# A mixture-of-experts stage on one Trainium2 core: narrow slots' tokens in one shared tile, a tenth ring buffer for weights, and block transposes placed behind the splits

## The chip, the cores and the metric

One core of one Trainium2 chip runs the whole program. The metric is device time in microseconds (us) of that core, from one launch; lower is better. PE is TensorE's matmuls, DVE is VectorE, ACT is ScalarE, SP issues nearly all transfers, POOL is idle in what follows.

## The reference, cut to what matters

Two layers of a trunk, 256 tokens of width 1024. The second layer ends in a mixture of eight experts, of which each token uses two:

```python
logits = (t @ w_router) + b_router
top_val, top_idx = lax.top_k(logits, 2)
top_w = jax.nn.softmax(top_val, axis=-1)
for e in range(8):
    out += combine[:, e:e+1] * ((silu(t @ w_gate[e]) * (t @ w_up[e])) @ w_down[e])
```

Each expert has a gate and an up matrix of 1024 x 3584 and a down matrix of 3584 x 1024, all f32. They are 352 MB together, of 470 MB that the kernel reads, and each weight is read once.

## The kernel before, in words

Everything up to the router runs first (some 520 us). Then comes the expert stage, written in one fixed order by hand, which each engine follows in program order.

**Slots and units.** Experts are ranked by how many tokens chose them. Eight slots hold them; `CAPS = (3, 4, 3, 3, 3, 2, 2, 2)` is the room of each slot in groups of 32 tokens. A slot's expert is cut into seven chunks of 512 hidden columns; one slot with one chunk is a *unit*. Slots run in two lanes, (0, 1, 2, 3) and (5, 6, 4, 7), whose units alternate. So slot 1 alternates with the last units of slot 5 and the first of slot 6.

**Pieces.** A unit needs four *pieces* of gate and up weights and two of down weights. A piece is 128 x 2048 f32, 1 MB, loaded by one DMA issue on SP (L137). The down matmuls of a unit (`ps_d`) stand on PE behind the gate and up matmuls (`ps_gu`) of the next unit.

**Narrow and wide.** Seven slots are *narrow* (2 or 3 groups). They stream the raw f32 pieces through PE in 32-column tiles (L1090). Slot 1, with 4 groups, is *wide*: each piece is first split into two fp32r parts, `hi` by a copy on ACT (L146) and `lo = raw - hi` by a subtraction on DVE (L154). Three matmuls then take each step: `hi` with both halves of the tokens (L260, L261), `lo` with one (L262). There are three `hi` and three `lo` buffers. A call `ahead(2)` behind the unit in front splits the first two pieces; the third and the fourth are split as the unit's own matmuls reach them.

**Between `ps_gu` and `ps_d`** a unit computes `sg = silu(gate)` on ACT (L1121) and `mh = up * sg` on DVE (L1124), and turns `mh` round: `h_T`. A narrow unit does that with 16 block transposes of 32 x 32 blocks on DVE (L1135), a wide one with four matmuls on PE (L1139). When a slot is done, `gated` scales its sums (`yg` on DVE L1173, `yhi` on ACT L1175, `ylo` on DVE L1176), and `combine` scatters them back (`ps_sc`, L1200).

**Where pieces land.** `need` loads pieces in the order of a plan. `mk` chooses the buffer of each. Nine `raw` buffers form a ring. Where no wide piece is within some items of the plan, the `hi` and `lo` buffers hold raw pieces too, 15 in all. Near the wide slot only the nine remain, and SP's next issue waits for the piece nine places before it to be used up (a narrow piece by its matmuls, a wide one by its `lo`).

**The 8 KB tiles.** Four buffers `a8` (8 KB on each partition) hold the gathered tokens of the slots at work (`xn` narrow, `xg` wide) and the running sum `macc`.

Of the kernel before, what the change touches and what calls it, by code (L numbers as in the profile page):

```python
# [17 lines left out]
P = 128  # L18
# [3 lines left out]
KT = 8  # L22
# [14 lines left out]
CAPS = (3, 4, 3, 3, 3, 2, 2, 2)  # L37
LANES = (0, 1, 2, 3), (5, 6, 4, 7)
STAGGER = 3
NR = NE - 1  # L40
EPS = 1e-6
NORM = D ** 0.5 / -8192.0
NEG = -1e30
G = 2048
# [9 lines left out]
def kernel(ctx, tc, x, cvec, wada, bada, wga, wqkv, wout, wfgu, wfd, wfd2,  # L54
# [5 lines left out]
    rawp = ctx.enter_context(tc.tile_pool(name="raw", bufs=RAW))  # L60
# [96 lines left out]
    plan = []  # L157
# [27 lines left out]
    def wide(e):  # L185
        return CAPS[e] == 4
# [9 lines left out]
    plan.append(down_chunk(*units[-1]))  # L196
    halves = [(k, s) for k, (_, n) in enumerate(plan) for s in range(0, n, G)]
    limit = [sum(k < first_gu for k, _ in halves)]
    raws, his, los, used = [], [], [], [0]

    def need(k):
        while len(raws) <= min(k, len(plan) - 1):
            i = len(raws)
            ap, n = plan[i]

            def mk(h):
                m = 2 * (i - first_gu) + h
                if m in SPARE8:
                    return pools["wk"], "a8", G
                if m in SPARE4:  # L210
                    return pools["wk"], "a4", G // 2
                if i >= first_gu and not any(n_ for _, n_ in plan[i - 6:i + 3]):
                    at = m % 15
                    return ((rawp, "raw", G), (hip, "hi", G), (lop, "lo", G))[(at >= 9) + (at >= 12)]
                return rawp, "raw", G

            raws.append(load(ap() if callable(ap) else ap, n or 4096, mk))

    def ahead(nhi, nlo=None, pre=True):

        for _ in range(nhi):
            if len(his) < limit[0]:
                k, s = halves[len(his)]
                need(k + pre)
                his.append(half_hi(raws[k], s))
            else:
                need(len(raws) + pre)
        for _ in range(nhi if nlo is None else nlo):
            if len(los) < limit[0]:
                k, s = halves[len(los)]  # L230
                los.append(half_lo(raws[k], s, his[len(los)]))
# [681 lines left out]
    def moe(acc, g_bc, mm, A, B, AW, bw):  # L913
# [45 lines left out]
        def shares():  # L959

            w0 = const.tile([P, NT], F32, name="w0")
            w1 = const.tile([P, NT], F32, name="w1")
            nc.vector.tensor_tensor(w1, m8[:, :, 1], m8[:, :, 0], op=ALU.subtract)
            nc.scalar.activation(w1, w1, AF.Exp)
            nc.vector.tensor_scalar(w0, w1, 1.0, None, op0=ALU.add)
            nc.vector.reciprocal(w0, w0)
            nc.vector.tensor_tensor(w1, w1, w0, op=ALU.mult)
            for t in range(NT):
                nc.vector.tensor_scalar(comb[:, t, :], oh[:, 1, t, :], w1[:, t:t + 1], None, op0=ALU.mult)
                nc.vector.scalar_tensor_tensor(comb[:, t, :], oh[:, 0, t, :], w0[:, t:t + 1], comb[:, t, :],  # L970
                                               op0=ALU.mult, op1=ALU.add)
# [67 lines left out]
        def dispatch(e, pm):  # L1039


            g, n = CAPS[e], 32 * CAPS[e]
            src, at = (gates, places) if e else (comb, posm)
            if wide(e):
                xg = a8("xg", [P, 2, KT, P], F32R)

                def put(js, f):
                    nc.scalar.activation(xg[:, 0, js, :], f, AF.Copy)
                    nc.vector.tensor_tensor(xg[:, 1, js, :], f, xg[:, 0, js, :].bitcast(F32), op=ALU.subtract)
            else:  # L1050
                xg = a8("xn", [P, KT, n])

                def put(js, f):
                    nc.vector.tensor_copy(xg[:, js, :], f)

            gather(pm, n, put)
            ps = bank("ps_ws")
            ws = sm.tile([P, 4], F32, tag="ws", name="ws")

            for tt in range(NT):  # L1060
                nc.tensor.matmul(ps[:, tt * P:(tt + 1) * P], at[:, tt, e:e + 1].to_broadcast([P, P]), ident,
                                 start=True, stop=True)
            if wide(e):
                for tt in range(NT):
                    nc.tensor.matmul(ps[:, S:S + 1], pm[:, 0, tt, :], src[:, tt, e:e + 1], start=tt == 0,
                                     stop=tt == NT - 1)
                pT = a4("pmT", [P, S], F32R)
                nc.vector.tensor_scalar(pT, ps[:, 0:S], spot[:, 0:1], None, op0=ALU.is_equal)
                nc.vector.tensor_copy(ws[:, 0:1], ps[:, S:S + 1])
                return xg, pT, ws  # L1070
            for t in range(g):
                for tt in range(NT):
                    for j in range(4):
                        nc.tensor.matmul(ps[32 * j:32 * j + 32, S + t:S + t + 1], pm[:, 0, tt, 32 * t:32 * t + 32],
                                         src[:, tt, e:e + 1], start=tt == 0, stop=tt == NT - 1)
            pT = a4("pmT", [P, g, S], F32R)
            for t in range(g):
                nc.vector.tensor_scalar(pT[:, t, :], ps[:, 0:S], spot[:, 4 + t:5 + t], None, op0=ALU.is_equal)
            nc.vector.tensor_copy(ws[:, 0:g], ps[:, S:S + g])
            return xg, pT, ws  # L1080
# [212 lines left out]
            nc.gpsimd.memset(room[:, at[0]:at[-1] + 1], 32.0 * v)  # L1293
        pm = slot_pick(0)
        shares()
        disp, accs = {0: dispatch(0, pm)}, {}
        idx_i, over_i = rank()
        ada_through(len(ada_order))
# [3 lines left out]
        with tc.manual_schedule():  # L1302
            limit[0] = len(halves)
            for r in range(NR):
                order[r + 1] = nc.values_load(idx_i[0:1, r:r + 1], engines=[mybir.EngineType.SP], min_val=1, max_val=NR,
                                              skip_runtime_bounds_check_because="a rank's expert")
            g2r = const.tile([P, 256], F32, tag="crep", name="g2r")
            pend, done = None, []
            for n, (e, c) in enumerate(units):
                early = [(pe, gated(pe)) for pe in done]  # L1310
                done = []
                if c == N_DN - 2 and e in after:
                    nxt = after[e]
                elif n == STAGGER - 1:
                    nxt = LANES[1][0]
                else:
                    nxt = None
                if nxt is not None:
                    pm = slot_pick(nxt)

                def between():
                    if pend and wide(pend[0]):
                        ahead(2)

                hm = gu_mm(e, between)
                if n == 1:
                    g2_bc = bcast(vec(1, 5), "g2bc")
                    dgs = [a2("dg", [P, 4, P]) for i in range(2)]
                    for i, dg in enumerate(dgs):
                        nc.vector.tensor_tensor(dg, ident[:, None, :].to_broadcast([P, 4, P]),  # L1330
                                                vec(1, 5)[:, 4 * i:4 * i + 4, None].to_broadcast([P, 4, P]), op=ALU.mult)
                    ps = bank("ps_g2")
                    for j in range(4):
                        nc.tensor.matmul(ps[32 * j:32 * j + 32, 0:256], ones_1[:, 0:32],
                                         dgs[j // 2][:, 2 * (j % 2):2 * (j % 2) + 2, :].rearrange("p a s -> p (a s)"),
                                         start=True, stop=True)
                    nc.scalar.activation(g2r, ps[:, 0:256], AF.Copy)
                for pe, ys in early:
                    if pe == 0:
                        macc = a8("macc", [P, NT, D])  # L1340
                    combine(pe, ys)
                if pend is not None:
                    if pend[1] == 0:
                        accs[pend[0]] = [accbank(f"ps_d{b}") for b in range((CAPS[pend[0]] + 1) // 2)]
                    dn_mm(*pend)
                    if pend[1] == N_DN - 1:
                        done.append(pend[0])
                if n + 1 < len(units) and wide(units[n + 1][0]):
                    ahead(2)
                pend = e, c, h_T(hm, CAPS[e], wide(e))  # L1350
                if nxt is not None:
                    disp[nxt] = dispatch(nxt, pm)
            for pe in done:
                combine(pe, gated(pe))
            dn_mm(*pend)
            combine(pend[0], gated(pend[0]), store)
# [164 lines left out]
```

## Time and profile before

| | before |
|---|---|
| median of 3 runs | 1393.73 us (1391.57 to 1395.06) |
| the profiled execution | 1396.89 us, of which the span of its instructions is 1395.2 us |
| PE busy, of the span | 1322.7 us (95%) |
| DVE / ACT busy | 772.2 us (55%) / 371.5 us (27%) |
| transfers | 473.64 MB, mean 339 GB/s |
| chain that ended last | PE 81%, DVE 8%, DMA 6%, ACT 4% |
| mean granted clock of PE | 0.983 |

Times in rows are us from the start of the span. The outside of the span is 1.7 us. Busy shares are means over stages with different limits, so the rows further down are taken stage by stage.

### The profile page before, as it was taken

How to read it: one execution, taken by the hardware profiler on the slowest of the kernel's cores; microseconds unless marked ns; L12 is line 12 of the kernel's file. 1: busy time of each engine (PE TensorE's matmuls, PEld its weight loads, DVE VectorE, ACT ScalarE, POOL GpSimd, SP SyncE). 2: the span in 40 equal slices, each digit the busy share in tenths (PEclk: the TensorE clock that was granted, in tenths of full speed). 3: DMA queues.
4: the chain of work that ended last, by engine and by line, in shares of the span. 5: the costliest groups of instructions: out<-in, count | busy, mean ns of one | idle time of the engine just before them, and what ended most of it. 6: DMA issues, size and time to landing. Idle time of an engine off the chain costs nothing.

```text
span 1395.2 us, 38875 instructions
## 1 busy us (share of the span) xinstructions
PE 1322.7 (95%) x17220; PEld 974.2 (70%) x17220; DVE 772.2 (55%) x1832; ACT 371.5 (27%) x574; POOL 3.1 (0%) x18
## 2 busy tenths in 40 slices
PE   4998999999899999999899999999999999999996
PEld 4877689999788676666567666766765776666663
DVE  3498677777689855343566565653344343334253
ACT  3336443443455430101234333410000100100000
POOL 0000000000000000000000000000000000000000
PEclk9999999999999999999999999999999999999999
DMA  9962787888461469899879999999999999999995
GB/s 387 399 276 91 262 305 275 307 300 300 161 237 59 151 218 401 353 424 424 344 309 423 387 373 371 367 413 424 424 425 424 424 424 424 396 418 418 423 424 215
DMA packets 66383, 473.64 MB, mean 339 GB/s; under 512 B 7840, under 2 KB 7968, under 8 KB 9248
## 3 DMA queue, kind: packets, MB, share of 16 engines
q1 hardware_dynamic: 66208, 471.09, 83.9%
q8 instruction: 137, 2.24, 0.6%
q14 instruction: 38, 0.31, 0.1%
HBM read 470.01 MB, written 1.05 MB: 338 GB/s over the span
## 4 chain that ended last, share of the span: by engine, by line
PE 81%; DVE 8%; DMA 6%; ACT 4%; issue 1%; SPq 0%; ACTq 0%; DVEq 0%
PE ps_gu L1090 28%; PE ps_d L1090 14%; PE ps_ga L262 4%; PE ps_ga L260 4%; PE ps_ga L261 4%; DMA raw<-in_wmd 3%; DVE lo L154 3%; PE ps_g L1031 2%; PE ps_y L714 2%; PE ps_ada L314 2%; DVE hT L1135 1%; PE ps_f L261 1%; PE ps_f L260 1%; PE ps_f L262 1%; PE ps_gu L262 1%; DMA raw<-in_wmgu 1%
## 5 line engine op out<-in xcount | busy, mean ns | idle before, releaser
L1090 PE MATMUL ps_gu<-raw,xn 128*32 128x256 f32 x8064 | 445.8, 379 | 1.2 <-DVE rt L983 0.6
L1090 PEld LDWEIGHTS ps_gu<-raw,xn 128*32 128x32 f32 x8064 | 279.3, 110 | 156.1 <-issue 2.4
L154 DVE TENSOR_TENSOR lo<-raw,hi 128x2048 fp32r<-128x2048 f32 x99 | 225.4, 2290 | 75.3 <-ACT hi L146 74.3
L1124 DVE TENSOR_TENSOR mh<-ps_gu,sg 128x256 f32<-128x256 f32 (+1 forms) x91 | 32.6, 382 | 368.5 <-ACT sg L1121 368.5
L1090 PE MATMUL ps_d<-raw,hT 128*32 128x256 f32 x4032 | 228.2, 379 | 2.4 <-DMA raw<-in_wmd 2.4
L146 ACT ACTIVATE hi<-raw 128x2048 fp32r<-128x2048 f32 x99 | 188.3, 1913 | 114.4 <-PE ps_ga L262 42.9
L1135 DVE STREAM_TRANSPOSE hT<-mh 32x96 f32<-32x96 f32 (+1 forms) x784 | 200.1, 255 | 13.2 <-PE ps_bc L379 0.2
L1090 PEld LDWEIGHTS ps_d<-raw,hT 128*32 128x32 f32 x4032 | 136.1, 110 | 84.9 <-DMA raw<-in_wmd 3.7
L1121 ACT ACTIVATE sg<-ps_gu 128x256 f32<-128x256 f32 (+1 forms) x91 | 31.9, 351 | 579.7 <-PE ps_gu L1090 511.8
L260 PE MATMUL ps_ga<-hThi,lo 128*128 128x256 f32 x480 | 137.9, 287 | 7.5 <-ACT hThi L452 7.5
L262 PE MATMUL ps_ga<-hTlo,hi 128*128 128x256 f32 x480 | 137.0, 285 | 0.5 <-DVE hTlo L457 0.5
L261 PE MATMUL ps_ga<-hThi,hi 128*128 128x256 f32 x480 | 136.5, 284 | 0.0
L260 PEld LDWEIGHTS ps_ga<-hThi,lo 128*128 128x128 f32 x480 | 93.2, 194 | 8.6 <-ACT hThi L452 8.4
L262 PEld LDWEIGHTS ps_ga<-hTlo,hi 128*128 128x128 f32 x480 | 92.5, 193 | 1.3 <-DVE hTlo L457 1.3
L261 PEld LDWEIGHTS ps_ga<-hThi,hi 128*128 128x128 f32 x480 | 92.8, 193 | 0.2
L550 DVE SCALAR_TENSOR_TENSOR cv<-zp,cols_sb,cv 128x256 f32<-128x256 f32 x206 | 85.6, 482 | 0.0
L262 PE MATMUL ps_gu<-lo,xg 128*128 128x512 f32 x112 | 46.3, 414 | 8.9 <-DVE lo L154 8.9
L260 PE MATMUL ps_gu<-hi,xg 128*128 128x512 f32 x112 | 46.3, 413 | 3.7 <-ACT hi L146 3.7
L353 DVE SCALAR_TENSOR_TENSOR ada_acc<-raw,cs,ada_acc 128x512 f32<-128x512 f32 x63 | 47.3, 750 | 1.2
L261 PE MATMUL ps_gu<-hi,xg 128*128 128x512 f32 x112 | 45.7, 408 | 0.0
L314 PE MATMUL ps_ada<-raw,crep 128*32 128x128 f32 x960 | 34.2, 301 | 7.5 <-DMA raw<-in_wada 7.2
L314 PEld LDWEIGHTS ps_ada<-raw,crep 128*32 128x32 f32 x960 | 28.9, 121 | 11.4 <-issue 8.5
(265 smaller groups left out, 1274.4 us busy)
## 6 DMA issues: line engine op xcount, KB each, us to landing
raw<-in_wmgu SPq DMA_DIRECT2D x222, 1024.0 KB, 13.7
raw<-in_wmd SPq DMA_DIRECT2D x111, 1024.0 KB, 14.3
raw<-in_wada SPq DMA_DIRECT2D x48, 1024.0 KB, 6.6
raw<-in_wfgu SPq DMA_DIRECT2D x22, 1024.0 KB, 5.9
raw<-in_wqkv SPq DMA_DIRECT2D x12, 1024.0 KB, 6.8
raw<-in_wfd SPq DMA_DIRECT2D x11, 1024.0 KB, 6.9
raw<-in_wga SPq DMA_DIRECT2D x8, 1024.0 KB, 11.2
raw<-in_wout SPq DMA_DIRECT2D x8, 1024.0 KB, 7.2
```

The lines of the kernel that those rows point to most:

```text
L146: nc.scalar.activation(hi[:, i * w:(i + 1) * w], r, AF.Copy)
L154: nc.vector.tensor_tensor(lo[:, w], r, hi[:, w].bitcast(F32), op=ALU.subtract)
L260: nc.tensor.matmul(o_, a[1], b[0], start=first, stop=False)
L261: nc.tensor.matmul(o_, a[0], b[0], start=False, stop=False)
L262: nc.tensor.matmul(o_, a[0], b[1], start=False, stop=last)
L314: nc.tensor.matmul(ps[32 * g:32 * g + 32, 0:P], crep[:, j, :], w(j)[:, g * P:(g + 1) * P], start=j == 0, stop=j == KT - 1)
L353: nc.vector.scalar_tensor_tensor(accs[ch], ws[ch](j), cs[:, j:j + 1], accs[ch], op0=ALU.mult, op1=ALU.add)
L550: nc.vector.scalar_tensor_tensor(cv[:, a, :], zp[:, a, i:i + S], cw[:, a, i:i + 1], cv[:, a, :], op0=ALU.mult, op1=ALU.add)
L1090: nc.tensor.matmul(ps[t // 2][32 * j:32 * j + 32, t % 2], x(t), w(j), start=first and t % 2 == 0, stop=last, skip_group_check=True)
L1121: nc.scalar.activation(sg[:, 2 * b:2 * b + m, :], v[:, 0:m, 0, :], AF.Silu)
L1124: nc.vector.tensor_tensor(hm[:, 2 * b:2 * b + m, :], v[:, 0:m, 1, :], sg[:, 2 * b:2 * b + m, :], op=ALU.mult)
L1135: nc.vector.transpose(hT[32 * q:32 * q + 32, :, j], v[32 * j:32 * j + 32, :, q])
```

## The change

Three edits, all in the expert stage:

1. One 8 KB tile, `home`, holds the tokens of the narrow slots 0, 2, 4, 5, 6 and 7 at fixed columns (`HOME`); slots that share columns follow each other in time. Slot 3 still takes a tile of its own.
2. The room that this frees in `a8` goes to raw pieces: near the wide slot every tenth piece goes there, elsewhere every sixteenth. The rings are thus 10 and 16 long, before 9 and 15.
3. Where a narrow unit stands in front of a wide one, its `h_T` (the 16 block transposes) is no longer issued at the end of that unit, but from `between()` in the wide unit, behind all four of its splits. This applies to seven units.

```diff
+HOME = (0, None, 0, None, 768, 768, 1536, 1536)
...
-                if i >= first_gu and not any(n_ for _, n_ in plan[i - 6:i + 3]):
-                    at = m % 15
-                    return ((rawp, "raw", G), (hip, "hi", G), (lop, "lo", G))[(at >= 9) + (at >= 12)]
-                return rawp, "raw", G
+                if i < first_gu + 6:
+                    return rawp, "raw", G
+                turn[0] += 1
+                if any(n_ for _, n_ in plan[i - 6:i + 3]):
+                    return (rawp, "raw", G) if turn[0] % 10 else (pools["wk"], "a8", G)
+                at = turn[0] % 16
+                return ((rawp, "raw", G), (hip, "hi", G), (lop, "lo", G), (pools["wk"], "a8", G))[
+                    (at >= 9) + (at >= 12) + (at >= 15)]
...
-                xg = a8("xn", [P, KT, n])
+                xg = a8("xn", [P, G]) if HOME[e] is None else home[:, HOME[e]:HOME[e] + KT * n]
+                xg = xg[:, 0:KT * n].rearrange("p (k n) -> p k n", k=KT)
...
+        home = a8("xn", [P, G])
         disp, accs = {0: dispatch(0, pm)}, {}
...
-            pend, done = None, []
+            pend, done, late = None, [], []
...
                 def between():
                     if pend and wide(pend[0]):
                         ahead(2)
+                    if late:
+                        late.append(h_T(late.pop(), CAPS[pend[0]]))
...
+                if late:
+                    pend = *pend[:2], late.pop()
                 if pend is not None:
...
                 if n + 1 < len(units) and wide(units[n + 1][0]):
                     ahead(2)
-                pend = e, c, h_T(hm, CAPS[e], wide(e))
+                if not wide(e) and n + 1 < len(units) and wide(units[n + 1][0]):
+                    late.append(hm)
+                    pend = e, c, None
+                else:
+                    pend = e, c, h_T(hm, CAPS[e], wide(e))
```

Only DVE's order changes; PE, ACT and SP issue the same instructions in the same order (their buffers differ). At the second wide unit the others' pattern shows (two of them have a few small DVE steps of the next slot in between as well). Here is DVE from the narrow unit's `mh` in front of it to the wide unit's two `mh`, before:

```order
L1124 TENSOR_TENSOR mh<-ps_gu_7119,sg 128x256
L154 TENSOR_TENSOR lo<-raw,hi 128x2048 x2
L1135 STREAM_TRANSPOSE hT<-mh 32x2x32 x16
L154 TENSOR_TENSOR lo<-raw,hi 128x2048 x2
L1124 TENSOR_TENSOR mh<-ps_gu_7255,sg 128x256
L1124 TENSOR_TENSOR mh<-ps_gu_7256,sg 128x256
```

and the same place of the changed kernel:

```order
L1130 TENSOR_TENSOR mh<-ps_gu_7118,sg 128x256
L155 TENSOR_TENSOR lo<-raw,hi 128x2048 x4
L1141 STREAM_TRANSPOSE hT<-mh 32x2x32 x16
L1130 TENSOR_TENSOR mh<-ps_gu_7237,sg 128x256
L1130 TENSOR_TENSOR mh<-ps_gu_7238,sg 128x256
```

The transposes moved behind the third and fourth split and stand right in front of the wide unit's `mh`.

At the first wide unit slot 0 has just ended, and its `yg` and `ylo` stand in the same place. DVE before:

```order
L154 TENSOR_TENSOR lo<-raw,hi 128x2048 x2
L1135 STREAM_TRANSPOSE hT<-mh 32x2x32 x16
L1173 SCALAR_TENSOR_TENSOR yg<-ps_d_5313,ws,g2r 128x256 x2
L1173 SCALAR_TENSOR_TENSOR yg<-ps_d_5314,ws,g2r 128x256
L1176 TENSOR_TENSOR ylo<-yg,yhi 128x768
L154 TENSOR_TENSOR lo<-raw,hi 128x2048 x2
```

and of the changed kernel:

```order
L155 TENSOR_TENSOR lo<-raw,hi 128x2048 x2
L1179 SCALAR_TENSOR_TENSOR yg<-ps_d_5313,ws,g2r 128x256 x2
L1179 SCALAR_TENSOR_TENSOR yg<-ps_d_5314,ws,g2r 128x256
L1182 TENSOR_TENSOR ylo<-yg,yhi 128x768
L155 TENSOR_TENSOR lo<-raw,hi 128x2048 x2
L1141 STREAM_TRANSPOSE hT<-mh 32x2x32 x16
```

Here the transposes moved behind `yg`, `ylo` and both splits.

## Rows read from the trace of the kernel before

**Rows 1.** Busy time by stretch; clock, DMA share and GB/s stand last.

```profile
675.00:925.00 250.00, 236.02 (x2400) 167.16 (x2396) 154.30 (x236) 98.12 (x90) 0.00 (x0) 0.97 0.91 368
925.00:1350.00 425.00, 425.00 (x7788) 279.22 (x7782) 159.68 (x558) 28.23 (x78) 0.00 (x0) 1.00 1.01 421
```

**Rows 2.** What PE waited for, 675 to 925: total, times, longest.

```profile
PE ps_gu L262 <- DVE lo L154: 8.9, 6, 2.3
PE ps_gu L260 <- ACT hi L146: 3.7, 1, 3.7
PE ps_sc L1200 <- DVE mh L1124: 1.3, 1, 1.3
```

**Rows 3.** What PE waited for, 925 to the end.

```profile
PE ps_d L1090 <- DMA raw<-in_wmd: 2.4, 2, 1.2
PE ps_gu L1090 <- DMA raw<-in_wmgu: 0.6, 1, 0.6
```

**Rows 4.** PE timeline, second wide unit: start, length, instruction, idle before it.

```profile
729.20 0.50 PE L262 MATMUL ps_gu<-lo,xg 128*128 128x512 f32 x1 [1.45 <-DVE lo L154]
...
734.53 0.85 PE L1090 MATMUL ps_d<-raw,hT 128*32 128x256 f32 x11
```

**Rows 5.** ACT timeline, the same unit's third and fourth `hi`.

```profile
721.49 1.92 ACT L146 ACTIVATE hi<-raw 128x2048 fp32r<-128x2048 f32 x1 [0.88 <-PE ps_d L261]
724.29 1.92 ACT L146 ACTIVATE hi<-raw 128x2048 fp32r<-128x2048 f32 x1 [0.88 <-PE ps_gu L261]
```

**Rows 6.** DVE timeline, the same unit.

```profile
722.85 2.21 DVE L1135 STREAM_TRANSPOSE hT<-mh 32x64 f32<-32x64 f32 x9
724.83 2.00 DVE L1135 STREAM_TRANSPOSE hT<-mh 32x64 f32<-32x64 f32 x8
726.85 4.49 DVE L154 TENSOR_TENSOR lo<-raw,hi 128x2048 fp32r<-128x2048 f32 x2
```

**Rows 7.** DVE timeline, first wide unit.

```profile
684.40 3.98 DVE L1135 STREAM_TRANSPOSE hT<-mh 32x64 f32<-32x64 f32 x16
688.40 1.27 DVE L1173 SCALAR_TENSOR_TENSOR yg<-ps_d,ws,g2r 128x256 f32<-128x256 f32 x3
...
692.37 4.49 DVE L154 TENSOR_TENSOR lo<-raw,hi 128x2048 fp32r<-128x2048 f32 x2 [0.84 <-ACT hi L146]
```

**Rows 8.** PE timeline, the same unit.

```profile
692.39 0.79 PE L260 MATMUL ps_gu<-hi,xg 128*128 128x512 f32 x1 [3.73 <-ACT hi L146]
694.72 0.79 PE L262 MATMUL ps_gu<-lo,xg 128*128 128x512 f32 x1 [1.11 <-DVE lo L154]
701.90 0.50 PE L1200 MATMUL ps_sc<-yhi,pmT 32*128 32x256 f32 x4
```

**Rows 9.** Busy time in pieces of 5 us, columns as in rows 1.

```profile
690.00:695.00 5.00, 1.50 (x3) 0.79 (x4) 3.59 (x3) 4.41 (x4) 0.00 (x0) 0.70 0.90 380
695.00:700.00 5.00, 5.00 (x15) 3.90 (x16) 2.20 (x2) 0.00 (x0) 0.00 (x0) 0.62 0.88 313
700.00:705.00 5.00, 5.00 (x65) 4.11 (x67) 1.79 (x4) 0.38 (x1) 0.00 (x0) 1.00 0.28 115
...
810.00:815.00 5.00, 3.96 (x20) 3.26 (x21) 4.57 (x7) 0.90 (x1) 0.00 (x0) 0.65 1.01 426
```

**Rows 10.** SP's queue, two issues behind each other in the same stretch.

```profile
696.90 0.33 SPq L137 DMA_DIRECT2D raw<-in_wmgu  x1
708.28 4.51 SPq L137 DMA_DIRECT2D raw<-in_wmgu  x3
```

**Rows 11.** PE timeline, sixth wide unit.

```profile
859.08 0.66 PE L262 MATMUL ps_gu<-lo,xg 128*128 128x512 f32 x1 [2.29 <-DVE lo L154]
865.97 3.66 PE L1090 MATMUL ps_d<-raw,hT 128*32 128x256 f32 x64
```

**Rows 12.** The chain that ended last, its end: start, length, what.

```profile
1359.72 19.58 DMA raw<-in_wmd
...
1379.35 3.67 PE ps_d L1090 x60
```

More of the change, by code (lines that the diff above doesn't have):

```diff
@@ L198 @@
     limit = [sum(k < first_gu for k, _ in halves)]
-    raws, his, los, used = [], [], [], [0]
+    raws, his, los, used, turn = [], [], [], [0], [0]
     def need(k):
```

## The prediction, on record before the changed kernel ran

> **What bounds the kernel now.** I read the busy time by stretch first. From 925 to 1350 PE is busy in all 425 us and the transfers run at 421 GB/s with a share of 1.01; from 675 to 925, where slot 1 runs, PE is busy in 236 of 250 us and the transfers move 368 GB/s [rows 1]. The reader is to see two resources full at once in the long stretch, and neither full in the stretch before it. Next, the waits of PE. Between 675 and 925 they are 13.9 us: 8.9 us in six waits for a `lo`, 3.7 us for one `hi`, 1.3 us for a `mh` [rows 2]. After 925 PE waits 3.0 us for transfers in all [rows 3], and the chain that ended last shows where: the last pieces land at 1379.3 and PE has 3.7 us of matmuls left [rows 12]. So the end is set by both: PE's idle time near slot 1 delays all that follows, and at the tail the transfers are 3.0 us behind PE. A gain must move both.
>
> **The transposes, second wide unit.** PE waits 1.45 us for its third `lo`, until 729.20 [rows 4]. That `lo` could have begun when its `hi` was ready, at 721.49 + 1.92 = 723.41 [rows 5]. DVE was in the transposes from 722.85 to 726.83, and the two `lo` (4.49 us, 2.25 each) followed at 726.85 [rows 6]. With the transposes behind them, the third `lo` runs from 723.4 to 725.7. PE wants it at 729.20 - 1.45 = 727.75: the wait goes. The fourth `hi` is ready at 726.21, its `lo` at 728.5, one piece (some 2.7 us, half of 734.53 - 729.20) ahead of need. The transposes then take 728.5 to 732.5.
>
> What is late next? The narrow unit's `ps_d`, which needs them, stood at 734.53 [rows 4] and comes to 733.1 when 1.45 us go. The transposes finish 0.6 us before it. That is the cover of this edit, and thin. Queued behind them on DVE are the wide unit's two `mh`; the second needs the end of `ps_gu` anyway, and its reader on PE stands behind the narrow `ps_d` (some 3.6 us), so nothing waits.
>
> The five later waits for `lo` have the same pattern: 8.9 us less the first unit's 1.11 make **7.8 us**. One wide unit has no such wait, and there I book nothing.
>
> **The first wide unit.** Here `yg` stands behind the transposes, `yhi` behind `yg`, and ACT's third `hi` behind `yhi`: PE stood 3.73 us for the `hi` and 1.11 us for the `lo` [rows 8]. Without the 3.98 us of transposes [rows 7] all of that moves up by 3.98: the third `hi` is ready at 688.4, and its `lo`, which began at 692.37 [rows 7], runs from 688.4 to 690.7. PE can start the `hi` matmul where its idle time began, 692.39 - 3.73 = 688.66, and waits some 1.6 us for the `lo`. Gain **4.0 us**.
>
> **The clock.** PE's granted clock was 0.70 and 0.62 in the two 5 us pieces after that wait [rows 9]: half the time at the lower of its two levels, 1.2 GHz. From the `lo` matmul to the end of the unit PE took 701.90 - 694.72 = 7.18 us [rows 8]; the same part of the second wide unit, at full clock, took 734.53 - 729.20 = 5.33 us [rows 4]. If the clock stays up, **1.85 us** come back. In the sixth wide unit the wait of 2.29 us was followed by 865.97 - 859.08 = 6.89 us for the same part [rows 11]: **1.56 us** more. After the wait of 1.45 us in the second wide unit the clock stayed up, so I take it that it does after 1.6 us too. The wait for `mh` speaks against it: it was 1.3 us, and the clock behind it is 0.65 [rows 2, 9]. So the other bound is that 1.85 us are lost again.
>
> The Trainium skill ("TensorE: Matmul & The Clock Gate", Terms) prices low clock as its time multiplied by one less the granted share. By that rule the 6.8 us at half clock that rows 9 give for the first unit would cost 3.4 us, not 1.85, and the sum below would be 1.55 us larger. Part of that time PE stood idle anyway, so the measured difference stands.
>
> Sum for PE: 7.8 + 4.0 + 1.85 + 1.56 = **15.2 us** earlier at 925.
>
> **The tenth buffer and the shared tile.** The transfers must come earlier as well, or the gain is lost where they are full. Near slot 1 they are not full: SP issued a piece at 696.90 and the next at 708.28 [rows 10], and the rate fell to 115 GB/s meanwhile [rows 9]. SP waited for the piece nine places back, which PE used up in `ps_d`. Such releases are PE's and DVE's own steps, so they move up with PE. With ten buffers each issue waits for the piece ten places back, so at each such stop one piece more is on its way. A piece at the full rate takes 1.049 MB / 421 GB/s = 2.5 us. When the transfers turn full (about 920 before) they are then 15.2 + 2.5 = **17.7 us** earlier. At the leave from the ring of ten to that of 16 SP has a few more issues to wait for than before; I book nothing, and take 3 us as the other bound. The 16th buffer helps only where the transfers are not full after 925, which is hardly anywhere [rows 1]: nothing.
>
> The shared tile removes no instruction and adds none; the slots that are at work together have columns of their own. A false wait of one slot's copies for another's matmuls would cost at most the 1.3 us that a `mh` cost here [rows 2] at each of four hand-overs, 5 us; I take nothing.
>
> **The sum.** PE can end 15.2 + 3.0 = 18.2 us earlier, since it need not wait at the tail; the transfers 17.7 us. The later one counts: 17.7 us. The profiled execution took 1396.89 us, so 1379.2; the median of the runs shown lies 3.2 us below it, so **1376.0 us**.
>
> **The rivals.** *The transfers set the end, and only the buffer counts.* The stretch from 925 on is full on the transfers' side [rows 1]. If their restarts near slot 1 do not move up, all that PE gains turns into waits for pieces further on; 2.5 us remain, 1391 us, no change by this kernel's measurement (0.3%, 4 us, is about what can be told). Against it: the restarts wait for PE's and DVE's releases [rows 10]. The Trainium skill ("Perfetto Trace Analysis", Identifying the Most-Contended Engine) says that gains come from the most contended engine, and has transfers judged by their rate from memory. By that rule this rival holds, since the transfers are the fullest. The trace agrees for 925 to 1350, not for the 250 us before.
>
> *Slower: the transposes arrive late for `ps_d`.* They now stand behind the fourth `lo`. If the third and fourth `lo` do not come earlier (because `hi` or the raw piece is late), the fourth ends at 726.85 + 4.49 = 731.3, the transposes at 735.3, and PE, at 734.53, waits 0.8 us; with the clock falling after it, by the 1.56 us above, 2.4 us in each of seven units: 17 us, 1410 us at worst, about 1399 us if the clock holds. It decides from 0.6 us of delay on. Against it: `hi` three and four waited for PE's own matmuls [rows 5], not for pieces.
>
> *Half of it.* The margin of 0.6 us fails in some units, or the clock falls again in the first, or the leave costs its 3 us: 6 to 9 us are taken back, 1384 us.
>
> *More.* The stretch of low clock behind the wait for `mh` [rows 2, 9] goes too, as PE comes to it differently: 1.3 us of wait and some 2 of clock (as in the first wide unit), 1372 to 1373 us. Its own queue on DVE is not changed, so this is unlikely.
>
> **How the numbers follow.** As summed, within some 4 us: 0.60. Half: 0.16. More: 0.10. Transfers alone, no change: 0.08. Slower: 0.06. The likeliest time is 1376; its own range is 1372 to 1381. Eight in ten needs the cases of half and of more in it, with the runs' own spread of 3.5 us: 1369 to 1388. Faster 0.86, within 0.3% 0.08, slower 0.06.
>
> **What would show it.** In the changed kernel's profile: PE's waits for `lo` near slot 1 fall from 8.9 to about 1.6 us, and the one for `hi` (3.7) goes; PE is at full clock there but for the stretch behind the `mh` wait; the transposes end before `ps_d` starts, and no wait of `ps_d` for `hT` appears; the rate of the transfers near slot 1 is over 385 GB/s; the waits for pieces after 925 fall below 1 us. I would be wrong if `ps_d` waited for `hT`, if waits for pieces appeared around 1000 to 1020, or if the granted clock fell in other places.

## The result, and the profile after

The changed kernel ran in 1378.13 us (median of 4 runs, 1375.44 to 1382.62), the kernel before beside it in 1394.39 us (1391.57 to 1399.99, 4 runs): a ratio of 0.9881, 95% interval 0.9854 to 0.9908: 1.2% faster, clear of noise. The profiled execution took 1380.11 us, its span 1378.4 us (before: 1395.2). A later set of six runs gave 0.988 [0.9852, 0.9909] again.

Runs of one kernel differ by up to 10 us, and the profiles show that part of this arises ahead of the expert stage, which nothing in the change touches. So the profiles are also compared from the first matmul of the expert stage to the last matmul. These are two rows of PE's timeline of the kernel before (start, length, instruction):

```profile
521.84 1.07 PE L1090 MATMUL ps_gu<-raw,xn 128*32 128x256 f32 x16
...
1386.59 0.40 PE L1200 MATMUL ps_sc<-ylo,pmT 32*128 32x256 f32 x4
```

and the same two of the changed kernel:

```profile
522.06 1.07 PE L1096 MATMUL ps_gu<-raw,xn 128*32 128x256 f32 x16
...
1369.71 0.40 PE L1206 MATMUL ps_sc<-ylo,pmT 32*128 32x256 f32 x4
```

Before: 1386.59 + 0.40 - 521.84 = 865.1 us. After: 1369.71 + 0.40 - 522.06 = 848.0 us, and in two further profiles of the changed kernel 847.1 and 846.8. Below, this is called the **expert time**. Of the change it shows 17.8 us (865.1 less the mean of the three, 847.3).

Busy time by stretch of the changed kernel, as in [rows 1] (PE, PEld, DVE, ACT, POOL; then clock, DMA share, GB/s):

```profile
675.00:910.00 235.00, 232.08 (x2444) 165.50 (x2440) 155.27 (x236) 98.10 (x90) 0.00 (x0) 0.99 0.98 399
910.00:1335.00 425.00, 424.85 (x7779) 279.54 (x7775) 161.65 (x562) 28.27 (x78) 0.00 (x0) 1.00 1.01 420
```

PE now stands 2.9 us in the stretch of slot 1, where it stood 14.0 us [rows 1], and the transfers run at 399 GB/s there instead of 368. What PE waited for in that stretch, and then from 910 to the end (total, times, longest):

```profile
PE ps_gu L267 <- DVE lo L155: 1.6, 1, 1.6
PE ps_sc L1206 <- DVE mh L1130: 1.3, 1, 1.3
...
PE ps_d L1096 <- DMA raw<-in_wmd: 2.4, 2, 1.3
...
PE ps_gu L1096 <- DMA raw<-in_wmgu: 0.7, 1, 0.7
```

Against [rows 2], five of six waits for `lo` and the one for `hi` are gone. Against [rows 3], the waits for pieces at the end have stayed: 3.1 us, before 3.0 (two further profiles of the changed kernel have 2.5 and 2.6).

DVE at the second wide unit, as in [rows 6], and behind it the PE row that needs the transposes:

```profile
718.29 2.29 DVE L155 TENSOR_TENSOR lo<-raw,hi 128x2048 fp32r<-128x2048 f32 x1 [0.51 <-ACT hi L147]
721.09 2.29 DVE L155 TENSOR_TENSOR lo<-raw,hi 128x2048 fp32r<-128x2048 f32 x1 [0.51 <-ACT hi L147]
723.29 4.03 DVE L1141 STREAM_TRANSPOSE hT<-mh 32x64 f32<-32x64 f32 x16
...
727.66 1.72 PE L1096 MATMUL ps_d<-raw,hT 128*32 128x256 f32 x28
```

The `lo` now wait for their `hi` (0.51 us each) and not for the transposes. The transposes end at 723.29 + 4.03 = 727.32, and `ps_d` begins at 727.66: a margin of 0.34 us, with no wait.

The granted clock in pieces of 5 us, the place of [rows 9] first (columns as above):

```profile
690.00:695.00 5.00, 4.06 (x17) 3.31 (x18) 4.89 (x11) 0.63 (x2) 0.00 (x0) 1.00 1.01 423
695.00:700.00 5.00, 5.00 (x66) 4.12 (x68) 4.49 (x13) 0.38 (x1) 0.00 (x0) 1.00 0.95 398
...
805.00:810.00 5.00, 5.00 (x17) 3.96 (x16) 2.36 (x2) 1.91 (x1) 0.00 (x0) 0.69 1.01 424
```

Where the clock was 0.70 and 0.62 it is 1.00. One stretch at the lower level is left, behind the wait for `mh`.

### The profile page after: what moved, and what is told of

The parts are those of the page before. It is cut to its first block, busy times and chain, and to the rows that moved or that the text cites. A ratio compares the mean times of both kernels' runs of the same rounds, so it can differ in the third digit from the quotient of the medians.

```text
span 1378.4 us, 38871 instructions
## 1 busy us (share of the span) xinstructions
PE 1316.5 (96%) x17220; PEld 971.7 (70%) x17220; DVE 773.1 (56%) x1832; ACT 371.4 (27%) x574; POOL 3.1 (0%) x18
## 4 chain that ended last, share of the span: by engine, by line
PE 81%; DMA 8%; DVE 6%; ACT 3%; issue 1%; SPq 0%; ACTq 0%; DVEq 0%
PE ps_gu L1096 26%; PE ps_d L1096 13%; DMA raw<-in_wmd 4%; PE ps_ga L267 4%; PE ps_ga L265 4%; PE ps_ga L266 4%; DMA raw<-in_wmgu 3%; PE ps_g L1036 2%; PE ps_y L719 2%; PE ps_gu L267 2%; PE ps_gu L265 2%; PE ps_gu L266 2%; DVE cv L555 2%; PE ps_ada L319 2%; DVE lo L155 1%; PE ps_f L265 1%
## 5 line engine op out<-in xcount | busy, mean ns | idle before, releaser
L265 PE MATMUL ps_gu<-hi,xg 128*128 128x512 f32 x112 | 44.5, 397 | 0.0
L266 PE MATMUL ps_gu<-hi,xg 128*128 128x512 f32 x112 | 44.1, 394 | 0.0
```

Of the source, the lines that this page charges most:

```text
L265: nc.tensor.matmul(o_, a[1], b[0], start=first, stop=False)
L266: nc.tensor.matmul(o_, a[0], b[0], start=False, stop=False)
```

## The experiments

Expert time of every profile, in us, in one table; what each kernel is follows below. The third column is the part of it behind slot 1, from PE's transposes of `mh` in the last wide unit to the last matmul. A low clock near slot 1 does not enter that part.

| kernel | expert time | of it behind slot 1 | low clock behind the `mh` wait |
|---|---|---|---|
| before | 865.1 | 483.0 | yes, 6.8 us |
| buffers only | 865.0 | 482.8 | yes, 6.8 us |
| order only | 846.0 | 483.0 | no |
| the change | 848.0, 847.1, 846.8 | 483.5, 482.5, 482.2 | yes, 3.4 us, in all three |
| combine behind the down matmuls | 849.7 | 482.3 | no `mh` wait; 6.8 us behind a `lo` wait |
| leave mended | 844.6; 845.9 | 481.5; 481.4 | no; yes, 3.4 us |
| order only, `mh` ahead | 844.6 | 483.0 | no wait |
| leave mended, `mh` ahead | 842.3, 842.6 | 480.7, 481.0 | no wait |
| transposes later | 882.0 | 481.2 | yes, 3.4 us |

**The order alone.** The kernel before with the third edit and nothing else:

```diff
...
+                    if late:
+                        late.append(h_T(late.pop(), CAPS[pend[0]]))
...
+                if not wide(e) and n + 1 < len(units) and wide(units[n + 1][0]):
+                    late.append(hm)
+                    pend = e, c, None
...
```

> The kernel before with the move of the transposes alone; rings of 9 and 15, no shared tile. Theory (the order carries the gain, the buffer none of it): PE's waits for lo near slot 1 fall from 8.9 to 1.6 us, the one for hi goes, no waits for pieces appear there; 15 to 17 us below the kernel before, as the full change. Rival (the order needs the tenth buffer): in the kernel before pieces landed down to some 1.4 us ahead of their split, so with PE 7 us earlier at the second wide unit and a ring of nine, splits or PE wait for pieces near slot 1, over 3 us in all, and the kernel is at least 3 us slower than the full change.

Measured: 1376.94 us (1373.92 to 1380.03), ratio 0.9883 [0.986, 0.9906]. PE's waits in the stretch of slot 1, and at the end:

```profile
PE ps_gu L262 <- DVE lo L154: 1.6, 1, 1.6
PE ps_sc L1200 <- DVE mh L1124: 1.3, 1, 1.3
...
PE ps_d L1090 <- DMA raw<-in_wmd: 2.4, 2, 1.2
```

They are those of the whole change. The gain is 18.1 us between the medians, above the 15 to 17 expected, and 19.2 us in expert time: 1.3 us more than the change gains, whose low clock behind the `mh` wait this profile does not have. The order carries the gain; that the transfers would swallow it without a tenth buffer has fallen.

**The buffers alone.** The changed kernel without the third edit (`h_T` stays at the end of its unit; `HOME`, the tenth and the sixteenth buffer remain):

```diff
-                if not wide(e) and n + 1 < len(units) and wide(units[n + 1][0]):
-                    late.append(hm)
-                    pend = e, c, None
-                else:
-                    pend = e, c, h_T(hm, CAPS[e], wide(e))
+                pend = e, c, h_T(hm, CAPS[e], wide(e))
```

> The changed kernel with the transposes back at the end of their own unit; shared tile and rings of 10 and 16 stay. Theory: the waits for lo and hi stay at 8.9 and 3.7 us; 0 to 2.5 us below the kernel before (one piece at the full rate at most). Rival (the buffer carries a good part): 5 us or more below the kernel before.

Measured: 1392.98 us (1389.7 to 1398.19), ratio 0.9989 [0.997, 1.0007]. The waits of [rows 2] are all there:

```profile
PE ps_gu L267 <- DVE lo L155: 8.9, 6, 2.3
PE ps_gu L265 <- ACT hi L147: 3.7, 1, 3.7
```

The expert time is 0.1 us below that of before. Without the new order, the buffers bring nothing that can be measured. Beside it they bring little: behind slot 1 the change took 482.7 us on the mean of three profiles, the order alone 483.0.

**The leave mended.** The *leave* is the place near the end of slot 1 where the ring of ten ends and that of sixteen begins. This is the changed kernel, and the first piece that may lie in the ring of sixteen is put on a `hi` buffer, which is free, instead of on a `raw` buffer still in use:

```diff
...
                 if any(n_ for _, n_ in plan[i - 6:i + 3]):
+                    near[0] = True
                     return (rawp, "raw", G) if turn[0] % 10 else (pools["wk"], "a8", G)
+                if near[0]:
+                    near[0], turn[0] = False, 9
                 at = turn[0] % 16
...
```

> The changed kernel, with the count that picks buffers set so that the first piece behind the wide slot goes to a hi buffer, as it happened to be in the kernel before. Theory (the tenth buffer's lead was lost at the leave from the ring of ten, where SP waited for raw buffers that were still in use): the rate near 900 to 925 rises, the last pieces land 2 to 2.5 us earlier against PE, the waits for pieces at the tail fall from 3.1 us to under 1.2 us, and the kernel is 2 to 2.5 us below the changed kernel, some 18 to 19 us below the one before. Rival (the lead is lost elsewhere, or the tail does not depend on it): waits at the tail stay near 3 us, same time as the changed kernel.

Measured: 1374.42 us (1371.76 to 1375.63), ratio 0.9855 [0.9832, 0.9878]. Run once more, beside the changed kernel itself and the two kernels further down:

> The mended leave alone, once more beside the changed kernel on the same chip: 2 us (the lead that is lost) to 3.7 us (the medians so far) below it by the theory; equal to it if the first difference was one of the runs and not of the kernels.

> The changed kernel itself, once more, on the same chip as the two runs beside it, so that they are compared at the same time: 1375 to 1382 us, ratio 0.986 to 0.991. If it comes out at 1374 us or below, the gain of the mended leave (3.7 us between the medians so far) was not one.

Measured: 1374.3 us (1372.92 to 1378.5), ratio 0.9855 [0.9829, 0.9882], and the changed kernel 1381.25 us (1374.33 to 1383.41), ratio 0.988 [0.9852, 0.9909]. The intervals overlap, and the 7 us between these medians lie in part ahead of the expert stage (last section), so the trace has to decide. SP's queue in the changed kernel where the ring changes (start, length of the group, issues):

```profile
905.48 0.91 SPq L138 DMA_DIRECT2D raw<-in_wmd  x2
910.66 9.42 SPq L138 DMA_DIRECT2D raw<-in_wmgu  x4
920.28 1.07 SPq L138 DMA_DIRECT2D raw<-in_wmd  x2
```

and in the second profile of the mended leave:

```profile
902.22 0.91 SPq L138 DMA_DIRECT2D raw<-in_wmd  x2
903.33 1.91 SPq L138 DMA_DIRECT2D raw<-in_wmgu  x4
905.66 2.76 SPq L138 DMA_DIRECT2D raw<-in_wmd  x2
910.54 8.80 SPq L138 DMA_DIRECT2D raw<-in_wmgu  x4
```

In the one SP stands 9.42 us over four issues, in the other 1.91 us. The four issues of gate and up pieces after those take 8.80 us in the mended kernel too: what it gains is that SP gets ahead by one such group. The transfers' rate from 900 to 925 in the changed kernel, then in the mended one, then with the order alone (last column):

```profile
900.00:925.00 25.00, 25.00 (x433) 15.07 (x436) 10.58 (x30) 2.10 (x4) 0.00 (x0) 1.00 0.99 406
```

```profile
900.00:925.00 25.00, 25.00 (x440) 15.06 (x432) 11.51 (x40) 1.05 (x3) 0.00 (x0) 1.00 1.01 424
```

```profile
900.00:925.00 25.00, 25.00 (x436) 15.05 (x432) 11.50 (x39) 1.05 (x3) 0.00 (x0) 1.00 1.01 426
```

So the change slows the transfers at a place where, with the old rings, they were not slowed (its two other profiles have 399 and 406 GB/s, the first of the mended leave 425; in 25 us counted from the same matmul, all six profiles with the longer rings and without the mend lie at 398 to 407, the seven others at 424 to 426). 25 us at 18 GB/s less are 0.45 MB, which at 424 GB/s is 1.1 us of transfers lost at this place alone. The expert time says 1.4 us (845.9 against 847.3, both with the low clock behind `mh`), the part behind slot 1 says 1.3 us (481.4 and 481.5 against a mean of 482.7, no overlap). That is some two thirds of the 2 to 2.5 us expected. The waits for pieces at the end, expected below 1.2 us, are 2.5 us in the first profile and 1.8 in the second:

```profile
PE ps_d L1099 <- DMA raw<-in_wmd: 1.8, 2, 1.1
```

The changed kernel's three profiles have 3.1, 2.5 and 2.6 us. So these waits fell by 0.6 us on the mean, and the rest of the gain came further ahead: from PE's first scatter into `ps_sc` for slot 1 to the next one, about 100 us later, the mended kernel took 98.5 us in both profiles, the changed one 99.8, 98.5 and 98.9, the order alone 99.4.

**The combine behind the down matmuls.** The changed kernel, with the combine of a finished slot issued behind the unit's `dn_mm`, so that PE no longer meets the `mh` wait in front of its scatter:

```diff
+                behind = pend is not None and wide(pend[0])
                 for pe, ys in early:
...
-                    combine(pe, ys)
+                    if not behind:
+                        combine(pe, ys)
...
+                if behind:
+                    for pe, ys in early:
+                        combine(pe, ys)
```

> The changed kernel, with slot 5's scatter matmuls behind the wide unit's down matmuls instead of ahead of them, so that they need not wait for mh to free a PSUM bank. Theory (what PE gains near slot 1 moves the transfers' restarts too): the wait of 1.3 us for mh goes and with it the stretch of low clock behind it, 3 us below the changed kernel, waits for pieces at the tail stay near 3 us. Rival (the transfers set the end by themselves): the same time as the changed kernel, and the waits at the tail grow by as much as PE gained.

Measured: 1379.18 us (1377.42 to 1379.41), ratio 0.9892 [0.987, 0.9914]: no gain, and 849.7 us of expert time, 2.4 above the change. DVE and PE at the place:

```profile
803.11 2.48 DVE L1211 TENSOR_TENSOR macc<-macc,ps_sc 128x512 f32<-128x512 f32 x4 [4.55 <-PE ps_sc L1206]
805.51 6.69 DVE L155 TENSOR_TENSOR lo<-raw,hi 128x2048 fp32r<-128x2048 f32 x3
```

```profile
807.85 0.80 PE L267 MATMUL ps_gu<-lo,xg 128*128 128x512 f32 x1 [3.20 <-DVE lo L155]
```

The `mh` wait is gone, but DVE's additions into `macc` now wait for the later scatter (4.55 us idle), the next unit's `lo` stand behind them, and PE waits 3.20 us for a `lo`. The wait moved and grew; the step that failed is that nothing would stand behind the additions.

**Transposes one step later.** The changed kernel, with the 16 transposes behind the wide unit's `mh` instead of in front of it:

```diff
-                    if late:
-                        late.append(h_T(late.pop(), CAPS[pend[0]]))
...
                 hm = gu_mm(e, between)
+                if late:
+                    late.append(h_T(late.pop(), CAPS[pend[0]]))
```

> The change, with the transposes of a late unit put one step further: behind the wide unit's own `mh` instead of ahead of it. It tests the step that the transposes stand under cover in the changed kernel (they end 0.33 us before the down matmuls of `ps_d` that read them) and the price of losing that cover. Theory: the two `mh` multiplications come at the end of the wide unit's gate/up matmuls, so all 16 transposes (4.03 us) and the sg and mh of the wide unit (about 1.2 us) lie open on TensorE: about 4.9 us of wait on VectorE's hT before `ps_d` in each of the seven late units, 34 us in all, and behind each wait a stretch at a low clock (1.6 to 1.9 us each, 11 to 13 us in all). Nearly all of it is paid ahead of 925 us and goes to the end, since the transfers wait for the same buffers: 1378 + 34 + 12 = about 1424 us, range 1408 to 1430. Rival (the transfers set the end, TensorE has slack): the delay is mostly swallowed, below 1390 us, with the transfers getting ahead during the waits.

Measured: 1413.37 us (1411.63 to 1420.05), ratio 1.0144 [1.0115, 1.0173]. PE at the first and the second wide unit, and the 5 us behind the second:

```profile
698.66 1.71 PE L1096 MATMUL ps_d<-raw,hT 128*32 128x256 f32 x27 [1.37 <-DVE hT L1141]
...
731.01 2.36 PE L1096 MATMUL ps_d<-raw,hT 128*32 128x256 f32 x24 [4.06 <-DVE hT L1141]
```

```profile
730.00:735.00 5.00, 3.98 (x44) 2.10 (x48) 1.64 (x7) 0.00 (x0) 0.00 (x0) 0.66 0.77 324
```

Six waits are 4.06 us, the first is 1.37: 25.7 us in seven, not 34. The whole price in expert time is 882.0 - 847.3 = 34.7 us. Up to PE's transposes in the last wide unit it is 36.2 us (400.8 against 364.6 from the first matmul); behind slot 1, 1.5 us come back (481.2 against 482.7). So 36.2 - 25.7 = 10.5 us are left for the low clock, which followed the six long waits and not the short one, and for what each wait takes with it beyond its own length. So the theory held (the delay arrives at the end, all but 1.5 us), the time lies in the range stated, and the sum of 34 + 12 us was 11 us too high, 8 of them in the waits: of the six long waits the transposes' own 4.03 us account for nearly all, and the `sg` and `mh` of the wide unit are hidden. The 0.34 us of margin in the change guard some 35 us.

**`mh` ahead of one `lo`.** In the one unit with a combine in front of the down matmuls, the second `lo` is issued behind `mh`. First on top of the mended leave:

```diff
                     if pend and wide(pend[0]):
-                        ahead(2)
+                        ahead(2, 1 if early else 2)
...
                 hm = gu_mm(e, between)
+                if early and wide(pend[0]):
+                    ahead(0, 1)
```

> The leave of the ring mended (as in the run that sets the first piece behind a wide slot on a `hi` buffer), and besides, in the one unit where a combine stands between the gate/up matmuls and the down matmuls, only one of the two `lo` stands ahead of `mh` on VectorE, the other behind it. Theory: `mh` then follows its `sg` at once, the wait of TensorE before the scatter into `ps_sc` (1.3 us) falls below 0.2 us, the stretch at a low clock behind it (3.4 us, at 804.7 to 808.1 in the changed kernel) goes with it (about 1.6 us), the second `lo` is late by 0.5 us but not needed before 806 us. TensorE comes 2.9 us earlier at 925; as the lead of the transfers is kept there, 1.5 to 2.9 us of it arrive at the end: 1371.5 to 1373 us against 1374.4 of the mended leave alone. Rival 1: the low clock has its cause in the thin scatter matmuls and stays; then 1.3 us at most. Rival 2: the transfers set the end from 925 on and nothing arrives: 1374.4 us, with longer waits for pieces at the end.

> The mended leave with one `lo` behind `mh`, once more: 842 to 843.5 us from the first narrow matmul to the last, no stretch at the low clock between 650 and 1370 us. If it comes out at 845 us or above, the step of 2.3 to 3.6 us against the mended leave was one of the runs.

Measured: 1375.09 us (1371.48 to 1379.47), ratio 0.9856 [0.9831, 0.9882], beside the changed kernel's 1381.25; in a second set of runs 1373.2 us (1372.1 to 1377.23), ratio 0.9837 [0.98, 0.9874]. The first median lies above the 1371.5 to 1373 us expected; the expert time of the second, 842.6 us, lies in the 842 to 843.5 expected. DVE at the place, in the first:

```profile
795.64 2.29 DVE L155 TENSOR_TENSOR lo<-raw,hi 128x2048 fp32r<-128x2048 f32 x1 [1.11 <-ACT hi L147]
798.61 0.43 DVE L1133 TENSOR_TENSOR mh<-ps_gu,sg 128x256 f32<-128x256 f32 x1 [0.68 <-ACT sg L1130]
798.95 2.28 DVE L155 TENSOR_TENSOR lo<-raw,hi 128x2048 fp32r<-128x2048 f32 x1
```

`mh` now waits for its `sg` only. To price it, PE's transposes in the units on both sides of the place, start to start; the changed kernel:

```profile
792.27 0.66 PE L1145 MATMUL ps_hT<-ident,mh 128*128 128x128 f32 x4
802.45 0.50 PE L1206 MATMUL ps_sc<-yhi,pmT 32*128 32x256 f32 x3 [1.34 <-DVE mh L1130]
825.71 0.66 PE L1145 MATMUL ps_hT<-ident,mh 128*128 128x128 f32 x4
```

the first profile of the mended leave, with the same wait and the clock at full level behind it:

```profile
790.22 0.66 PE L1148 MATMUL ps_hT<-ident,mh 128*128 128x128 f32 x4
800.40 0.50 PE L1209 MATMUL ps_sc<-yhi,pmT 32*128 32x256 f32 x3 [1.34 <-DVE mh L1133]
822.13 0.66 PE L1148 MATMUL ps_hT<-ident,mh 128*128 128x128 f32 x4
```

and with `mh` ahead:

```profile
790.34 0.66 PE L1148 MATMUL ps_hT<-ident,mh 128*128 128x128 f32 x4
820.82 0.66 PE L1148 MATMUL ps_hT<-ident,mh 128*128 128x128 f32 x4
```

33.44, 31.91 and 30.48 us: the low clock costs 1.53 us and the wait 1.43. No low clock is left near slot 1 in either profile although the same scatter matmuls run, so rival 1, that they cause it by themselves, has fallen. In expert time it is 2.2 us below the mended leave without the low clock (842.45 against 844.6) and 3.5 below the one with it, so what PE gains there does arrive, and rival 2 has fallen too. The run times alone can't tell it from the mended leave (1375.09 and 1373.2 us against 1374.42 and 1374.3). In expert time, this version is 4.9 us below the change.

The same edit without any new buffer, on the order alone:

> The kernel before with the third edit alone (the late transposes), and with one `lo` behind `mh` in the unit with the combine: no new buffer at all. Counted from the first narrow matmul to the last matmul, since runs differ ahead of that point: the kernel before took 865.1 us, the changed kernel 848.0 and 847.1, the order alone 846.0, the mended leave 844.6 and 845.9, the mended leave with `mh` ahead 842.3. Theory (what is saved on TensorE ahead of 925 us arrives at the end as long as the transfers are not late; the tenth buffer and the ring of sixteen are worth 0 to 2 us): 843 to 845 us without the buffers. Rival (without the tenth buffer the slack of pieces near the wide slot, 0.3 us in the run of the order alone, is used up, and TensorE waits there): a wait for a piece of 1 us or more near 820 to 900 us, and 846 us or more.

Measured: 1374.19 us (1372.39 to 1380.55), ratio 0.983 [0.9795, 0.9864], expert time 844.6 us, and no wait for a piece near slot 1. The theory held. Against the same with buffers and mended leave (842.45) the buffers are worth 2.1 us, once the leave lets them, all of it behind slot 1: up to PE's transposes in the last wide unit both took 361.6 us.

A third profile of the changed kernel ran beside these:

> The changed kernel, a third profile beside the two: 847 to 848.5 us from the first narrow matmul to the last, with the 1.3 us wait for `mh` and, by the two profiles so far, a stretch of 3.4 us at the low clock behind it. Without that stretch (as in one of two profiles of the mended leave, with the same wait): about 846 us.

Measured: 1374.74 us, expert time 846.8 us (0.2 below the range), with the low clock behind `mh`.

## Why the prediction was right, and which step of it was not

**The time.** 1376.0 us forecast, 1378.13 measured; 17.7 us of gain forecast against the profiled execution; 17.8 measured in expert time, 16.8 between the profiled executions, 16.3 between the medians. That the sum came out so close is in part luck: it hides one step that failed and one term that was too small, and their errors, some 2.4 us each way, cancel.

**The waits.** As forecast: `lo` from 8.9 to 1.6 us, `hi` gone, no `ps_d` wait for `hT`. The margin of the transposes at the second wide unit was 0.34 us, not 0.6.

**PE's gain at 925, the term that was mis-sized.** 15.2 us were forecast. Here are PE's transposes in the last wide unit, in the kernel before and in the changed one:

```profile
903.97 0.66 PE L1139 MATMUL ps_hT<-ident,mh 128*128 128x128 f32 x4
```

```profile
886.63 0.66 PE L1145 MATMUL ps_hT<-ident,mh 128*128 128x128 f32 x4
```

From the first expert matmul that is 382.13 and 364.57 us: 17.6 us earlier. The first wide unit gave 5.4 us (4.0 + 1.85 forecast): its `lo` matmul came 4.0 us earlier and the stretch behind it took 5.34 us instead of 7.18, both as forecast, but the scatter matmuls that follow took 0.46 us longer. The five later waits gave 1.7, 1.7, 2.9, 4.1 and 1.7 us, 12.2 in all where 7.8 + 1.56 were booked. Each wait took some 0.3 us more with it than its own length, and in the unit of 2.9 us half of the low clock went: behind the `mh` wait it lasted 6.8 us before and 3.4 us now. The rival *more* had that place, at a tenth of the chance, and about half of it came true. Nothing in the edit was meant to do that, and the order alone had no low clock there at all, so this part is luck.

**The clock.** "I take it that it does after 1.6 us too" was right: 1.00 behind that wait [rows 9 against the profile after]. By the Trainium skill ("TensorE: Matmul & The Clock Gate", Terms), low clock costs its time multiplied by one less the granted share: an estimate of 1.7 us for 3.4 us at half share. Where PE was busy throughout, behind the `mh` wait, the rows give 1.53 us, so the trace nearly agrees; in the first wide unit, where PE also stood idle in part of the 6.8 us, that estimate is 3.4 us and the measured price 1.84.

**The tenth buffer, the step that failed.** "At the leave from the ring of ten to that of 16 [...] I book nothing" and "the waits for pieces after 925 fall below 1 us" were wrong. The term of 2.5 us, one more piece on its way when the transfers turn full, was lost at the leave. The changed kernel's SP stands 9.42 us over four issues there, the mended one's 1.91, and the rate there is 406 GB/s against 424. The buffers without the new order gave 0.1 us, against the 2.5 of the sum. With the leave mended they give 1.4 us over the order alone, or 2.1 with `mh` ahead. Why they give no more than that no run shows. The waits at the end stayed at 2.5 to 3.1 us in the three profiles of the change: the transfers moved up by about as much as PE did, and hardly further.

**The rivals.** *Only the buffer counts* fell: the order alone reached 0.9883, the buffers alone 0.9989. The Trainium skill ("Perfetto Trace Analysis", Identifying the Most-Contended Engine) says to optimize the engine of the highest occupancy first. The trace agrees in so far as what went was idle time of PE, busy for 95% of the span. But the instructions that moved stood on DVE, busy for 55%, and near slot 1 the transfers came earlier by it too. *Transposes late* did not happen, but its price is measured: 34.7 us when all the cover is gone. Why the waits at the end did not fall below 1.5 us even with the leave mended stays open. The last two waits for pieces end 4.9 us apart (1374.45 and 1379.35 before), and PE uses what landed in 3.7 us. So the transfers may fall behind there whatever the lead; no run tried to change that stretch.

## What to carry to other kernels

When two resources are full in one stretch and neither in the stretch before it, look at the order on a third, half idle engine in that earlier stretch: an instruction that nobody needs yet, in front of one that somebody waits for, cost 17.6 us of PE here by the change (19.1 by the order alone), clock included. The lead of a longer ring was lost here where the ring's length changes; look at the issuing queue and the transfers' rate at such a place. And where a wait is moved by putting work later, list what stands behind that work on its own engine first.

## What the runs showed of the hardware that was not expected

The same wait of PE, 1.34 us in front of the scatter into `ps_sc`, was followed by the low clock in seven of the nine profiles that have it (6.8 us before and with the buffers only; 3.4 us in three of the change, one of the mended leave and with the transposes later) and not in the two others (order alone, first of the mended leave). Waits of 1.6 us in the first wide unit were followed by it in none of eleven profiles. What PE did just ahead differs between the two places: 32-row scatter matmuls there, 128-row ones here. Behind the scatter it can't decide alone, since PE's instructions there are the same in all nine profiles and the clock fell in only seven; what does decide stays open.

Profiles of one kernel differ mostly ahead of the expert stage. Here are the stretch up to the first expert matmul and the last 26 us of it, in the third profile of the changed kernel (1373.0 us of span; PE's busy time stands second, the clock is the third number from the end):

```profile
0.00:518.06 518.06, 475.71 (x3788) 405.81 (x3788) 378.73 (x748) 228.46 (x365) 3.14 (x18) 0.98 0.66 250
492.00:518.00 26.00, 25.10 (x313) 22.07 (x311) 15.13 (x59) 8.97 (x23) 0.00 (x0) 1.00 0.63 228
```

and in its second (1381.7 us):

```profile
0.00:526.50 526.50, 483.17 (x3788) 412.76 (x3788) 378.57 (x748) 228.36 (x365) 3.14 (x18) 0.97 0.67 250
500.00:526.00 26.00, 25.09 (x292) 22.70 (x290) 14.30 (x57) 8.54 (x22) 0.00 (x0) 0.80 0.65 252
```

For the same 3788 instructions PE was busy 7.5 us longer in the second, and just ahead of the expert stage its clock was 0.80 instead of 1.00. The first expert matmul starts at 526.50 instead of 518.06 us. These 8.4 us are nearly all of the 8.7 between the spans, and more than the steps of 1 to 5 us that the later experiments had to tell apart.
